# Fewer ScalarE products for VectorE's convolution taps, and GpSimd's taps dealt out in other places

## The chip, the cores and the metric

The kernel runs on one core of a Trainium2 chip. A core has five engines that run their own queues in a fixed order and wait for each other by semaphores: TensorE (PE, with its weight loads as PEld), VectorE (DVE), ScalarE (ACT), GpSimd (POOL) and SyncE (SP), which issues most transfers. Data lies in SBUF, results of TensorE in the banks of PSUM. The metric is the device time of one execution in microseconds (us).

## The reference, cut to what matters

One decoder layer over 256 positions of width 1024. Two token mixers read the same normalized input `h`: a convolution module and sparse attention with 16 heads. The change touches the convolution; the attention runs next to it in time.

```python
def conv_module(u, dw_w, dw_b, ln_g, ln_b, pw_w):
    a, gt = jnp.split(u, 2, axis=-1)
    v = a * jax.nn.sigmoid(gt)
    v = lax.conv_general_dilated(                 # depthwise, causal, 31 taps, 1024 channels
        v, dw_w[:, None, :], window_strides=(1,), padding=((CONV_WIDTH - 1, 0),), ...) + dw_b
    v = jax.nn.silu(layer_norm(v, ln_g, ln_b))
    return v @ pw_w
...
y = jax.nn.sigmoid(g_conv) * conv_out + jax.nn.sigmoid(g_attn) * nsa_out
return y @ w_out
```

Cross-attention into 256 memory tokens and a SwiGLU feed-forward part follow; the change leaves them alone.

## The kernel before

**Chunks and halves.** All weights of the first projection come in chunks of 512 KB, in the order u, kc, vc, q, ks, kw, vs, vw, ga, gc (u is the convolution's input, kc to vw the attention's keys and values, ga and gc the two gates). Each chunk is cut into a rounded high half, by ScalarE (L187), and a low half, the rest (L190). GpSimd makes the low halves of the chunks up to ga3, VectorE those of gc and what follows. TensorE multiplies high by high, high by low and low by high (L279).

**The taps.** The eight blocks of 128 channels form four chains of two blocks: 0, 2, 4 and 6. A tap multiplies a shifted view of the input (`vt`) by one weight per channel and adds it to the chain's sum. `taps_v` does this on VectorE: either as a fused multiply and add for each block (L458), or ScalarE makes the product of both blocks (L442) into one of four buffers with the tag vw, and VectorE adds it in one instruction of twice the length (L454). The sum, `yp`, lies in PSUM. `taps_g` is GpSimd's: ScalarE makes a product (L472), or GpSimd itself for taps 5 and 11 (L470), into one of the same four buffers, and GpSimd adds it (L474). Chains 0, 2 and 4 are wholly VectorE's. Of chain 6 GpSimd has taps 0 to 15 and VectorE taps 16 to 30, and L478 joins the two parts on GpSimd. Then GpSimd forms the sum for the layer norm (L662, two L664, folded by L333).

**What sets the order.** `convolve(n_v, n_g, *marks)` takes the next n_v steps of VectorE's taps and n_g of GpSimd's, puts them behind the marks (the instructions named) and gives them a priority 1500 places later, so that they fill gaps. It is called once behind each chunk's result. A scheduler then simulates the engines and writes each engine's order down; nothing is reordered on the chip. Marks, priorities and durations thus decide where a tap stands in a queue.

**Attention.** Eight pairs of heads, each in two steps. `scores` of a pair: TensorE writes the scores of the first 128 queries of both heads into one PSUM bank with the tag s0, of which there is one, and those of the later 128 into banks of the tag s. VectorE adds the bias and takes minima: four L783 read s0, four L789 the others. `weights`: ScalarE takes exponentials with their sums (L804), VectorE makes factors of the sums (L807, L809) and multiplies them in, four L812 and four L814 in turn. Then TensorE transposes the result (L825): `pt_b` into the bank s0, `pt_a` into one of the two banks "pt". The program lets pair 1's scores go ahead of pair 0's transposes. So `pt_b` of pair 0 cannot be written before the last L783 of pair 1 has read the bank, and these L783 stand behind pair 0's L812 and L814 in VectorE's queue. Behind pair 0's transposes TensorE has the next gate chunk and pair 2's scores.

**The gates.** L698 takes the gate ga out of PSUM on ScalarE; the next gate's matmuls need that bank.

Of the kernel before, what the change touches and what calls it, by code (L numbers as in the profile page):

```python
# [11 lines left out]
AF = mybir.ActivationFunctionType  # L12
# [10 lines left out]
TAPS = 31  # L23
# [78 lines left out]
def tile_hybrid_block(  # L102
# [15 lines left out]
    nc = tc.nc  # L118
# [18 lines left out]
    def small(name, shape, dt=F32, tag=None, bufs=1):  # L137
        return sb.tile(shape, dt, tag=tag or name, name=name, bufs=bufs)
# [10 lines left out]
    def aux(name, shape, tag, bufs):  # L149
        return axp.tile(shape, F32, tag=tag, name=name, bufs=bufs)  # L150

    def f(ap):
        return ap.bitcast(F32)
# [17 lines left out]
    def col(base, j):  # L171
        return ppt[:, base + j:base + j + 1]
# [22 lines left out]
    first, splits, apart = {}, {}, {}  # L195
# [25 lines left out]
    def behind(*marks):  # L221

        stack = ExitStack()
        for m in marks:
            stack.enter_context(tc.issue_after(m.ins))
        return stack
# [63 lines left out]
    def gemm(name, x, nat=False):  # L290

        ps = bank(f"ps_{name}")
        for i in range(2):
            sweep(ps, halved(name, i), x, i, nat, name in in_order)
        return ps
# [122 lines left out]
    for i in range(4):  # L418
        hs = slice(2 * i, 2 * i + 2)
        for kb in (2 * i, 2 * i + 1):  # L420
            vec = nc.vector.scalar_tensor_tensor(out=hf[:, kb], in0=xt_t[:, kb], scalar=col(PP_GMIX, kb),
                                                 in1=r1, op0=ALU.mult, op1=ALU.mult)
# [16 lines left out]
    def product_of(j, t, to):  # L439

        for i in range(2):
            nc.scalar.activation(to[:, i], vt[j + i][:, t:t + S], AF.Identity, scale=col(PP_DW + TAPS * (j + i), t),  # L442
                                 bias=col(PP_DB, j + i) if t == 0 else 0.0)

    def taps_v(j, ts, out):

        acc = aux(f"yp{j}", [P, 2, S], "pt", 2)
        product_of(j, ts[0], acc)
        for n, t in enumerate(ts[1:]):
            to = out if t == ts[-1] else acc  # L450
            if n % 2:
                pr = small(f"vw{j}_{t}", [P, 2, S], tag="vw", bufs=4)
                product_of(j, t, pr)
                nc.vector.tensor_tensor(out=to, in0=acc, in1=pr, op=ALU.add)  # L454
                yield
                continue
            for i in range(2):
                nc.vector.scalar_tensor_tensor(out=to[:, i], in0=vt[j + i][:, t:t + S], scalar=col(PP_DW + TAPS * (j + i), t),  # L458
                                               in1=acc[:, i], op0=ALU.mult, op1=ALU.add)
                yield  # L460
# [36 lines left out]
    def convolve(n_v, n_g, *marks):  # L497

        here = tc.cur_priority
        tc.cur_priority = here + 1500  # L500
        with behind(*marks):
            for _ in range(n_v):
                next(on_v, None)
            for _ in range(n_g):
                next(on_g, None)
        tc.cur_priority = here

    small("gap2", [P, 32])
    for j in range(NB):
        ps = gemm(f"u{j}", h)  # L510
        sg = small(f"sg{j}", [P, S], tag="sg", bufs=3)
        act = nc.scalar.activation(sg, ps[:, 1], AF.Sigmoid)
        vec = nc.vector.tensor_tensor(out=vt[j][:, PAD:], in0=ps[:, 0], in1=sg, op=ALU.mult)
# [41 lines left out]
    for kv, name in enumerate(("kc", "vc")):  # L555
        ps = gemm(name, h)
        zin = zins[:, kv]
        nc.vector.memset(zin[:, :, :, NCMP:], 0.0)
        for odd in range(2):
            for lo, g in ((0, 0), (64, 1)):  # L560
                at = (PP_POS if lo == 64 * odd else PP_SOP) + 16 * kv
                view = ps[lo:lo + 64, :, odd:S]
                vec = nc.vector.tensor_tensor(
                    out=zin[64 * odd:64 * odd + 64, :, g::2, 0:NCMP],
                    in0=bass.AP(tensor=view.tensor, offset=view.offset, ap=[list(view.ap[0]), [2, 16], [S, 2], [16, NCMP]]),
                    in1=ppt[lo:lo + 64, at:at + 16].unsqueeze(2).unsqueeze(3).to_broadcast([64, 16, 2, NCMP]), op=ALU.add)
        convolve(5, 0, vec)
    kcp = small("kcp", [P, GROUPS, 2, 16], F32R)
    vcs = small("vcs", [P, 2, HD], tag="sg", bufs=3)
    vals = long("vals", 12, (P, 2, HEADS * HD))  # L570
# [3 lines left out]
    def hidden():  # L574


        z_ps = aux("z_ps", [P, 64], "o", 1)
        for l in range(16):
            for kv in range(2):
                nc.tensor.matmul(z_ps[HD * kv:HD * kv + HD], lhsT=w1t[:, kv, l], rhs=zins[:, kv, l].rearrange("p g n -> p (g n)"),  # L580
                                 start=l == 0, stop=l == 15)
        zs = small("zs", [P, 64], tag="zs", bufs=2)
        nc.scalar.activation(zs, z_ps, AF.Sigmoid)
        nc.vector.tensor_tensor(out=zz[:HD, 0, :64], in0=z_ps[:HD], in1=zs[:HD], op=ALU.mult)
        nc.vector.tensor_tensor(
            out=zz[HD:, 1].rearrange("p (g r n) -> p g r n", g=GROUPS, r=4),
            in0=z_ps[HD:].rearrange("p (g n) -> p g n", g=GROUPS).unsqueeze(2).to_broadcast([HD, GROUPS, 4, 16]),
            in1=zs[HD:].rearrange("p (g n) -> p g n", g=GROUPS).unsqueeze(2).to_broadcast([HD, GROUPS, 4, 16]), op=ALU.mult)

    def compressed():  # L590

        kc_ps = aux("kc_ps", [P, GROUPS, 16], "s0", 1)
        nc.tensor.matmul(kc_ps, lhsT=ppt[:, PP_W2K:PP_W2K + P], rhs=zz[:, 0, :64].rearrange("p (g n) -> p g n", g=GROUPS),
                         start=True, stop=True)
        part(kcp[:, :, 0], kcp[:, :, 1], kc_ps[:])
        vc_ps = aux("vc_ps", [P, 2, HD], "o", 1)
        for i in range(2):
            nc.tensor.matmul(vc_ps[:, i], lhsT=zz[:, 1, i * P:i * P + P], rhs=ppt[:, PP_W2V:PP_W2V + HD],
                             start=True, stop=True)
        nc.scalar.activation(vcs, vc_ps, AF.Copy)  # L600
# [4 lines left out]
    for j in range(4):  # L605
        ps = gemm(f"q{j}", h)
        q0, q1 = ([qt[j // 2][:, 4 * (j % 2) + 2 * b + k] for b in range(2)] for k in range(2))
        for b in range(2):
            nc.scalar.activation(q0[b][0:64], ps[0:64, b], AF.Copy, scale=-0.125)
            act = nc.scalar.activation(q1[b][64:128], ps[64:128, b], AF.Copy, scale=-0.125)  # L610
        for b in range(2):
            nc.vector.scalar_tensor_tensor(out=q0[b][64:128], in0=ps[0:64, b], scalar=-0.125, in1=f(q0[b][0:64]),
                                           op0=ALU.mult, op1=ALU.subtract)
            vec = nc.vector.scalar_tensor_tensor(out=q1[b][0:64], in0=ps[64:128, b], scalar=-0.125, in1=f(q1[b][64:128]),
                                                 op0=ALU.mult, op1=ALU.subtract)
        convolve(7, 1, act, vec)
        with behind(*last):
            if j == 0:
                hidden()
            elif j == 2:  # L620
                compressed()
# [3 lines left out]
    for br, name in enumerate(("ks", "kw")):  # L625
        ps = gemm(name, h)

        for lo, g in ((0, 0), (64, 1)):
            for to in (lo, 64 - lo):
                act = nc.scalar.activation(kdh[to:to + 64, g::2, br], ps[lo:lo + 64], AF.Copy)  # L630
        for lo, g in ((0, 0), (64, 1)):
            for to in (lo, 64 - lo):
                vec = nc.vector.tensor_tensor(out=kdl[to:to + 64, g::2, br], in0=ps[lo:lo + 64],
                                              in1=f(kdh[lo:lo + 64, g::2, br]), op=ALU.subtract)
        convolve(5, 1, act, vec)


    for br, name in enumerate(("vs", "vw")):
        ps = gemm_nat(name, h)
        act = nc.scalar.activation(vst[:, :, br], ps, AF.Copy)  # L640
# [5 lines left out]
    g_ps = aux("g_ps", [P, S], "s0", 1)  # L646
    for kb in range(NB):
        nc.tensor.matmul(g_ps[64 * (kb % 2):64 * (kb % 2) + 64], lhsT=wg[:, kb], rhs=hf[:, kb], start=kb < 2, stop=kb >= NB - 2)
    sgn = small("sgn", [P, S], tag="sg", bufs=3)
    igd = small("igd", [P, HEADS, 2, 2])  # L650
    igc = small("igc", [P, 2, HEADS])
    convolve(8 * TAPS, 2, nc.scalar.activation(sgn, g_ps, AF.Copy))

# [35 lines left out]
    def gate(j, few=iter(())):  # L691

        ps = bank(f"ps_ga{j}")
        for i in range(2):
            for _ in rows(ps, halved(f"ga{j}", i), h, i):
                for _ in range(3):
                    next(few, None)
        return nc.scalar.activation(sga[:, 2 * j:2 * j + 2], ps, AF.Copy if j == 3 else AF.Sigmoid)  # L698
# [27 lines left out]
    for tb in range(2):  # L726
# [4 lines left out]
    vec = nc.vector.reciprocal(igd.rearrange("p h t b -> p t b h"),  # L731
                               sgt[:, :, HEADS:3 * HEADS].rearrange("p t (b h) -> p t b h", b=2))
    hm = cpt[:, CP_HM:CP_HM + 8].unsqueeze(2).to_broadcast([P, 8, HD])
    with behind(vec):
        for i in range(2):
            nc.vector.tensor_tensor(out=vcm[:, 8 * i:8 * i + 8], in0=vcs[:, i].unsqueeze(1).to_broadcast([P, 8, HD]), in1=hm,
                                    op=ALU.mult)
    convolve(0, TAPS, splits["ga1_0"][0])
    mark = gate(2)
    def compressed_weights(*marks):  # L740

# [699 lines left out]
```

## Time and profile before

| | |
|---|---|
| time, median of 3 runs (lowest to highest) | 543.54 us (543.37 to 545.13) |
| profiled execution, its own time | 544.06 us |
| its span, first to last instruction | 542.3 us |
| mean granted clock of TensorE | 0.991 |
| busy: PE, DVE, ACT, POOL | 527.9, 438.6, 380.4, 140.9 us |

The profile is of one execution, so sums are made against its own time. Busy time is per engine and counts no waiting. The timeline gives start and duration of each instruction and, in brackets, the idle time just ahead of it and what ended it; listed durations of neighbours on VectorE and ScalarE overlap a little. The granted clock is the share of full speed that the chip gave TensorE.

### The profile page before, as it was taken

To read this page: it belongs to the slowest core of one execution; us is meant where nothing else is said; L and a number is where in the kernel's file an instruction comes from. 1 tells how busy PE (TensorE), PEld (TensorE's weight loads), DVE (VectorE), ACT (ScalarE), POOL (GpSimd) and SP (SyncE) were. 2 spreads that over 40 slices of the span, in tenths; PEclk is the share of its full clock that TensorE was granted. 3 is DMA by queue.
4 is the path that set the end of the run, shared out by engine and by line. 5 is a ranking of instruction groups with operands and counts; after the bars stand their busy time and mean duration, and the time that the engine had idled before them with its cause. 6 is when DMAs were issued, how large, how long until landed. Compare 5 with 4: busy or idle time off the path is not lost.

```text
span 542.3 us, 11221 instructions
## 1 busy us (share of the span) xinstructions
PE 527.9 (97%) x4325; PEld 508.8 (94%) x4325; DVE 438.6 (81%) x841; ACT 380.4 (70%) x705; POOL 140.9 (26%) x101
## 2 busy tenths in 40 slices
PE   9999999999999499999999999999999999999995
PEld 8999999999999499898999999999999999988884
DVE  3885999678998999795777876498798887689996
ACT  3679895999988688789756685376465555567643
POOL 0009987888967400200001300040000000000002
PEclk9999999999999799999999999999999999999999
DMA  8946956543555144523576643438676555634502
GB/s 277 410 166 226 336 198 193 189 158 120 193 164 170 58 137 147 178 87 144 160 221 217 231 160 114 156 126 277 232 244 210 193 196 195 195 118 133 179 1 77
DMA packets 29301, 97.38 MB, mean 180 GB/s; under 512 B 3136, under 2 KB 5440, under 8 KB 28992
## 3 DMA queue, kind: packets, MB, share of 16 engines
q1 hardware_dynamic: 28672, 95.62, 52.9%
q10 hardware_dynamic: 576, 1.05, 0.5%
q8 instruction: 34, 0.56, 0.4%
q14 instruction: 19, 0.16, 0.1%
HBM read 95.41 MB, written 1.25 MB: 178 GB/s over the span
## 4 chain that ended last, share of the span: by engine, by line
PE 80%; ACT 11%; DVE 4%; DMA 3%; issue 1%; POOL 0%; SPq 0%; ACTq 0%; POOLq 0%
PE ps_f L279 22%; PE ps_u L279 8%; PE fo L1209 6%; PE ps_v L279 4%; PE ps_xq L279 4%; PE ps_pw L279 4%; PE ps_wo L279 4%; PE fos L1209 4%; ACT vw L442 3%; PE ps_gc L279 3%; PE ps_xo L279 3%; PE ps_k L279 2%; PE ps_q L279 2%; PE ps_xo L1094 2%; ACT vw L472 1%; DMA xtsq<-in_xt_dram 1%
## 5 line engine op out<-in xcount | busy, mean ns | idle before, releaser
L458 DVE SCALAR_TENSOR_TENSOR yp<-vt,ppt,yp 128x256 f32<-128x256 f32 x104 | 47.9, 484 | 3.9 <-ACT yp L442 2.5
L1278 POOL TENSOR_TENSOR x<-xs,gf 128x512 f32<-128x512 f32 x2 | 2.5, 1293 | 168.3 <-issue 168.3
L442 ACT ACTIVATE vw<-vt,ppt 128x256 f32<-128x256 f32 x104 | 44.6, 499 | 0.1
L279 PE MATMUL ps_f<-g,f_1h 128*128 128x256 f32 x352 | 44.4, 277 | 0.0
L279 PE MATMUL ps_f<-g,f_0h 128*128 128x256 f32 x352 | 43.9, 277 | 0.0
L279 PEld LDWEIGHTS ps_f<-g,f_1h 128*128 128x128 f32 x352 | 41.9, 188 | 0.0
L279 PEld LDWEIGHTS ps_f<-g,f_0h 128*128 128x128 f32 x352 | 41.8, 188 | 0.0
L187 ACT ACTIVATE f_0h<-f 128x1024 fp32r<-128x1024 f32 x22 | 23.3, 1058 | 17.8 <-issue 15.5
L804 ACT ACTIVATE p<-p,mins 128x128 f32<-128x128 f32 (+1 forms) x64 | 28.3, 444 | 10.2 <-DVE mins L783 10.0
L454 DVE TENSOR_TENSOR yp<-yp,vw 128x512 f32<-128x512 f32 x48 | 33.1, 695 | 2.2 <-ACT vw L442 0.9
L190 DVE TENSOR_TENSOR f_1l<-f,f_1h 128x1024 fp32r<-128x1024 f32 x22 | 27.3, 1246 | 4.9 <-ACT f_1h L187 4.9
L190 DVE TENSOR_TENSOR f_0l<-f,f_0h 128x1024 fp32r<-128x1024 f32 x22 | 27.3, 1243 | 3.9 <-ACT oxh L324 2.2
L187 ACT ACTIVATE f_1h<-f 128x1024 fp32r<-128x1024 f32 x22 | 23.2, 1059 | 8.2 <-PE ps_f L279 7.5
L279 PE MATMUL ps_f<-g,f_1l 128*128 128x256 f32 x176 | 23.6, 276 | 0.0
L1168 DVE TENSOR_TENSOR ab<-ps_f,rf 128x512 f32<-128x512 f32 x22 | 15.2, 689 | 10.4 <-PE ps_f L279 10.4
L279 PE MATMUL ps_f<-g,f_0l 128*128 128x256 f32 x176 | 23.6, 276 | 0.0
L474 POOL TENSOR_TENSOR yt<-yt,vw 128x512 f32<-128x512 f32 x15 | 20.2, 1348 | 12.0 <-ACT vw L472 10.8
L190 POOL TENSOR_TENSOR u_0l<-u,u_0h 128x1024 fp32r<-128x1024 f32 x5 | 12.0, 2406 | 40.0 <-ACT u_0h L187 40.0
L279 PEld LDWEIGHTS ps_f<-g,f_1l 128*128 128x128 f32 x176 | 21.6, 188 | 0.0
L279 PEld LDWEIGHTS ps_f<-g,f_0l 128*128 128x128 f32 x176 | 21.6, 188 | 0.0
L988 POOL COPY acc<-s_wo 128x256 f32<-128x256 f32 x1 | 0.7, 653 | 71.7 <-ACT s_wo L984 71.7
L1170 ACT ACTIVATE sl<-ab 128x256 f32<-128x256 f32 x22 | 9.1, 417 | 11.3 <-DVE ab L1168 11.3
(827 smaller groups left out, 1673.7 us busy)
## 6 DMA issues: line engine op xcount, KB each, us to landing
f<-in_wst_dram SPq DMA_DIRECT2D x44, 512.0 KB, 4.1
u<-in_wst_dram SPq DMA_DIRECT2D x14, 512.0 KB, 7.2
for<-in_wfo_dram SPq DMA_DIRECT2D x14, 512.0 KB, 3.8
q<-in_wst_dram SPq DMA_DIRECT2D x8, 512.0 KB, 5.8
ga<-in_wst_dram SPq DMA_DIRECT2D x8, 512.0 KB, 3.6
gc<-in_wst_dram SPq DMA_DIRECT2D x8, 512.0 KB, 3.5
v<-in_wst_dram SPq DMA_DIRECT2D x8, 512.0 KB, 4.1
pw<-in_wst_dram SPq DMA_DIRECT2D x8, 512.0 KB, 4.6
```

Of the source, the lines that this page charges most:

```text
L187: copies = [nc.scalar.activation(hi[:, at:at + n], w[:, at:at + n], AF.Copy) for at in range(0, shape[1], n)]
L190: low = eng.tensor_tensor(out=lo[:, at:at + n], in0=w[:, at:at + n], in1=f(hi[:, at:at + n]), op=ALU.subtract)
L279: mm = nc.tensor.matmul(ps[:, b], lhsT=lhsT, rhs=rhs, start=row + b + kb == 0, stop=kb == NB - 1 and row == 2 and b == 1)
L442: nc.scalar.activation(to[:, i], vt[j + i][:, t:t + S], AF.Identity, scale=col(PP_DW + TAPS * (j + i), t), bias=col(PP_DB, j + i) if t == ...
L454: nc.vector.tensor_tensor(out=to, in0=acc, in1=pr, op=ALU.add)
L458: nc.vector.scalar_tensor_tensor(out=to[:, i], in0=vt[j + i][:, t:t + S], scalar=col(PP_DW + TAPS * (j + i), t), in1=acc[:, i], op0=ALU.mu ...
L474: nc.gpsimd.tensor_tensor(out=y, in0=y, in1=pr, op=ALU.add)
L804: exp.append(nc.scalar.activation(t, t, AF.Exp, scale=-1.0, bias=mins[:, hd, qb, br:br + 1], accum_out=sums[:, hd, qb, br:br + 1]))
L1094: nc.tensor.matmul(qs[:, b], lhsT=parts[m, 1][wi][:, k, cs], rhs=x[xi][:, 4 + k], start=False, stop=k == 3 and row == 2 and b == 1)
L1168: nc.vector.tensor_tensor(out=ab, in0=ps, in1=rf.unsqueeze(1).to_broadcast([P, 2, S]), op=ALU.mult)
L1170: silu = nc.scalar.activation(sl, ab[:, 0], AF.Silu)
L1209: mm = nc.tensor.matmul(o[:, cs], lhsT=t[x], rhs=w[y][:, cs], start=start and n == 0, stop=stop and n == 2)
```

## The change

VectorE's chains take a product from ScalarE where n % 3 is 2, n being the tap's place behind the first: every third tap and no longer every second. The calls of `convolve` behind the chunks kc, vc, q, ks and kw take more steps of VectorE's taps and one or two of GpSimd's; the call behind the gate's logits takes all of GpSimd's steps that are left, and the later call behind ga1 is gone. (In the orders below, lines of the changed kernel behind that call are lower by one: L811 is L812 of before.)

```diff
@@ taps_v
-            if n % 2:
+            if n % 3 == 2:
                 pr = small(f"vw{j}_{t}", [P, 2, S], tag="vw", bufs=4)
@@ behind kc and vc
-        convolve(5, 0, vec)
+        convolve(8, 1, vec)
@@ behind q0 to q3
-        convolve(7, 1, act, vec)
+        convolve(8, 2, act, vec)
@@ behind ks and kw
-        convolve(5, 1, act, vec)
+        convolve(6, 1, act, vec)
@@ behind the gate's logits
-    convolve(8 * TAPS, 2, nc.scalar.activation(sgn, g_ps, AF.Copy))
+    convolve(8 * TAPS, TAPS, nc.scalar.activation(sgn, g_ps, AF.Copy))
@@ ahead of gate(2)
-    convolve(0, TAPS, splits["ga1_0"][0])
```

VectorE's queue around the normalizing of pair 0, before (yp is the sum in PSUM, here of chain 4; yt takes its last add):

```order
L190 TENSOR_TENSOR gc_0l<-gc_0_2614,gc_0h 128x1024
L458 SCALAR_TENSOR_TENSOR yp_1398<-vt_357,ppt,yp_1398 128x256
L454 TENSOR_TENSOR yt<-yp_1398,vw_30_1985 128x512
L807 SCALAR_TENSOR_TENSOR sums<-sums,igd 128x8
L809 RECIPROCAL sums<-sums 128x8
L812 TENSOR_SCALAR p_0_2280<-p_0_2280,sums 128x256
L814 TENSOR_SCALAR p_0_2265<-p_0_2265,sums 128x128
...
L814 TENSOR_SCALAR p_0_2265<-p_0_2265,sums 128x128
L783 ISA p_1_2439,mins<-s_1_2438,nb_2435 128x128
```

and after:

```order
L454 TENSOR_TENSOR yp_1467<-yp_1467,vw_27_1965 128x512
L458 SCALAR_TENSOR_TENSOR yp_1467<-vt_357,ppt,yp_1467 128x256
L806 SCALAR_TENSOR_TENSOR sums<-sums,igd 128x8
L458 SCALAR_TENSOR_TENSOR yp_1467<-vt_357,ppt,yp_1467 128x256
L808 RECIPROCAL sums<-sums 128x8
L458 SCALAR_TENSOR_TENSOR yp_1467<-vt_357,ppt,yp_1467 128x256
L811 TENSOR_SCALAR p_0_2244<-p_0_2244,sums 128x256
L813 TENSOR_SCALAR p_0_2229<-p_0_2229,sums 128x128
...
L813 TENSOR_SCALAR p_0_2229<-p_0_2229,sums 128x128
L458 SCALAR_TENSOR_TENSOR yp_1467<-vt_357,ppt,yp_1467 128x256
L454 TENSOR_TENSOR yt<-yp_1467,vw_30_1973 128x512
L782 ISA p_1_2403,mins<-s_1_2402,nb_2399 128x128
```

Chain 4's last add stood ahead of L807; now it stands behind the last L813, ahead of pair 1's first L782, with an L458. Two more L458 stand on either side of L808. Between the rows shown three more pairs of L812 and L814 (L811 and L813) follow.

GpSimd's queue from its last low half (ga_1l of ga3) on, before:

```order
L190 TENSOR_TENSOR ga_1l<-ga_1_2317,ga_1h 128x1024
L474 TENSOR_TENSOR yt<-yt,vw_8_1989 128x512
L474 TENSOR_TENSOR yt<-yt,vw_9_1993 128x512
L470 TENSOR_SCALAR vw_11_2178<-vt_358,ppt 128x256 x2
L474 TENSOR_TENSOR yt<-yt,vw_10_2174 128x512
L474 TENSOR_TENSOR yt<-yt,vw_11_2178 128x512
L474 TENSOR_TENSOR yt<-yt,vw_12_2182 128x512
L474 TENSOR_TENSOR yt<-yt,vw_13_2186 128x512
L662 TENSOR_TENSOR ysum<-yt 128x512
L474 TENSOR_TENSOR yt<-yt,vw_14_2190 128x512
L474 TENSOR_TENSOR yt<-yt,vw_15_2194 128x512
L478 TENSOR_TENSOR yt<-yt,part_364 128x512
```

and after:

```order
L190 TENSOR_TENSOR ga_1l<-ga_1_2281,ga_1h 128x1024
L474 TENSOR_TENSOR yt<-yt,vw_13_1914 128x512
L474 TENSOR_TENSOR yt<-yt,vw_14_1977 128x512
L662 TENSOR_TENSOR ysum<-yt 128x512
L474 TENSOR_TENSOR yt<-yt,vw_15_1981 128x512
L478 TENSOR_TENSOR yt<-yt,part_364 128x512
L664 TENSOR_TENSOR ysum<-ysum,yt 128x512 x2
L333 TENSOR_TENSOR ysum<-ysum 128x256
```

Behind the last low half stood eight L474 and an L470 pair; three L474 are left. The others moved up between the low halves of q to ga3. The join L478 and the layer norm's sum follow in both.

ScalarE's queue around pair 0's exponentials, before:

```order
L804 ACTIVATE p_0_2265,sums<-p_0_2265,mins 128x128 x3
L187 ACTIVATE gc_1h<-gc_1_2509 128x1024
L804 ACTIVATE p_0_2265,sums<-p_0_2265,mins 128x128
L472 ACTIVATE vw_12_2182<-vt_358,ppt 128x256 x2
L187 ACTIVATE gc_0h<-gc_0_2614 128x1024
L472 ACTIVATE vw_13_2186<-vt_358,ppt 128x256 x2
L698 ACTIVATE sga<-ps_ga_2286 128x512
L804 ACTIVATE p_0_2280,sums<-p_0_2280,mins 128x256 x2
```

and after:

```order
L472 ACTIVATE vw_14_1977<-vt_358,ppt 128x256 x2
L187 ACTIVATE gc_0h<-gc_0_2443 128x1024
L472 ACTIVATE vw_15_1981<-vt_358,ppt 128x256 x2
L698 ACTIVATE sga<-ps_ga_2163 128x512
L803 ACT_TABLE_LOAD
L803 ACTIVATE p_0_2229,sums<-p_0_2229,mins 128x128 x4
L187 ACTIVATE gc_1h<-gc_1_2473 128x1024
L187 ACTIVATE gc_0h<-gc_0_2578 128x1024
L698 ACTIVATE sga<-ps_ga_2250 128x512
L803 ACTIVATE p_0_2244,sums<-p_0_2244,mins 128x256 x2
```

The L472 pairs that stood between the exponentials of the earlier and the later queries have moved up; the two high halves of gc (L187) and L698 remain between them.

## The prediction

> **What bounds the kernel now.** I read three views in this order: the page's first part and the waits of PE, to see which engine sets the end and where it stops; then the timelines of PE, DVE and POOL around the one stop; then the granted clock by stretch. First the page's busy shares and, from the waits grouped by engine, PE's longest (total, times, longest):
>
> ```profile
> PE 527.9 (97%) x4325; PEld 508.8 (94%) x4325; DVE 438.6 (81%) x841; ACT 380.4 (70%) x705; POOL 140.9 (26%) x101
> PE pt_b L825 <- DVE mins L783: 7.0, 1, 7.0
> ```
>
> PE is busy 97% of the span, and half of what is missing is one wait: the transposes of attention pair 0 (pt_b) stand still until DVE has read the scores of pair 1 (L783) out of the PSUM bank that both use. ACT, DVE and POOL can lose work without any gain wherever PE does not wait. The timeline of PE around that wait, with the next pair's same work below it (start, duration):
>
> ```profile
> 175.01 1.07 PE L279 MATMUL ps_gc<-hh,gc_1h 128*128 128x256 f32 x8
> 183.05 1.08 PE L825 MATMUL pt_b<-cpt,p 128*128 128x128 f32 x4 [6.97 <-DVE mins L783]
> ...
> 188.59 0.40 PE L770 MATMUL s<-kdh,qt 128*128 128x512 f32 x1
> ...
> 193.63 1.08 PE L279 MATMUL ps_gc<-hl,gc_1h 128*128 128x256 f32 x8
> 194.55 0.60 PE L825 MATMUL pt_b<-cpt,p 128*128 128x128 f32 x4
> ...
> 195.86 0.38 PE L670 MATMUL mu<-ysum,ones 128*128 128x256 f32 x1
> ```
>
> From the stall's end to the next scores takes 188.59 - 183.05 = 5.54 us. At full clock the twelve transposes take 195.86 - 194.55 = 1.31 us and the two gemm groups of eight 0.91 each (such a group from 193.63 to 194.55), 3.13 in all. So 2.41 us more are lost behind the stall. The windows show why (length, busy time of PE, PEld, DVE, ACT and POOL, then the granted clock PEclk, third from the right):
>
> ```profile
> 176.00:181.00 5.00, 0.08 (x1) 0.00 (x0) 5.00 (x8) 1.10 (x2) 4.69 (x5) 1.00 0.00 0
> 181.00:183.00 2.00, 0.00 (x0) 0.00 (x0) 2.00 (x10) 0.70 (x4) 1.70 (x2) 0.54 0.00 0
> 183.00:188.00 5.00, 4.95 (x24) 4.98 (x25) 4.89 (x17) 4.83 (x17) 0.00 (x0) 0.50 0.36 112
> ```
>
> PE idles from 176.08, the clock is 1.00 until 181 and about 0.5 from there to 188: it fell some 5 us into the idle stretch. The place is worth 6.97 + 2.41 = 9.4 us.
>
> What held DVE is in its groups of 175:182, with POOL busy, against 183:200, with POOL idle (busy us, mean ns):
>
> ```profile
> L814 DVE TENSOR_SCALAR p<-p,sums 128x128 f32<-128x128 f32 x4 | 5.2, 1298 | 0.0
> ...
> L812 DVE TENSOR_SCALAR p<-p,sums 128x256 f32<-128x256 f32 x4 | 1.4, 353 | 0.0
> L814 DVE TENSOR_SCALAR p<-p,sums 128x128 f32<-128x128 f32 x4 | 1.1, 285 | 0.0
> L807 DVE SCALAR_TENSOR_TENSOR sums<-sums,igd 128x8 f32<-128x8 f32 x2 | 0.3, 159 | 0.0
> ```
>
> and the timelines of DVE and POOL there:
>
> ```profile
> 174.11 0.85 DVE L807 SCALAR_TENSOR_TENSOR sums<-sums,igd 128x8 f32<-128x8 f32 x1 [0.58 <-ACT p L804]
> ...
> 175.23 1.17 DVE L812 TENSOR_SCALAR p<-p,sums 128x256 f32<-128x256 f32 x1
> ...
> 181.98 0.28 DVE L783 CUSTOM_DVE_ANT_0 p<-s,nb 128x128 f32<-128x128 f32 x1
> ...
> 182.61 0.28 DVE L783 CUSTOM_DVE_ANT_0 p<-s,nb 128x128 f32<-128x128 f32 x1
> ...
> 174.95 2.63 POOL L474 TENSOR_TENSOR yt<-yt,vw 128x512 f32<-128x512 f32 x2
> ...
> 179.12 2.85 POOL L664 TENSOR_TENSOR ysum<-ysum,yt 128x512 f32<-128x512 f32 x2
> ```
>
> The eight normalizing instructions take 181.98 - 175.23 = 6.75 us beside POOL's adds. Four L814 lose 1.01 us each against the later pair, the first L812 0.82: 4.9 us in all. L807 loses 0.85 - 0.16, 0.7 more. They seem to start only where an instruction of POOL ends.
>
> **The change part by part.** The shares move first (page, groups):
>
> ```profile
> L458 DVE SCALAR_TENSOR_TENSOR yp<-vt,ppt,yp 128x256 f32<-128x256 f32 x104 | 47.9, 484 | 3.9 <-ACT yp L442 2.5
> ...
> L442 ACT ACTIVATE vw<-vt,ppt 128x256 f32<-128x256 f32 x104 | 44.6, 499 | 0.1
> ...
> L454 DVE TENSOR_TENSOR yp<-yp,vw 128x512 f32<-128x512 f32 x48 | 33.1, 695 | 2.2 <-ACT vw L442 0.9
> ```
>
> Chains 0, 2 and 4 have 30 taps behind the first: n % 2 gave ScalarE 15 of them, n % 3 gives 10. The 15 of chain 6 go from 7 to 4. So 18 taps leave ScalarE: 36 activations fewer, 18.0 us by 499 ns, for 36 more L458 on DVE (17.4 us by 484 ns) less 18 L454 (12.5 us by 695 ns): +4.9 us for DVE. Listed durations overlap by about 0.1, so by starts it is nearer +3. None of this is on PE's path by itself.
>
> L458's 484 ns is a mean over 104, most of them beside a busy POOL, so L458 does not wait for POOL as L814 does; if each of the 36 lost 1.0 us like L814, DVE would carry 36 us more. [...]
> DVE's extra is covered by the chunks' matmuls until 175, and would be paid in full if DVE were late there by itself.
>
> Second, POOL's taps. In the order of POOL shown ahead, five L474 and one L470 pair fewer stand behind its last low half (ga_1l). That last low half and what it must be early for:
>
> ```profile
> 152.79 2.46 POOL L190 TENSOR_TENSOR ga_1l<-ga,ga_1h 128x1024 fp32r<-128x1024 f32 x1
> 158.56 1.58 POOL L474 TENSOR_TENSOR yt<-yt,vw 128x512 f32<-128x512 f32 x1 [3.31 <-ACT vw L472]
> ...
> 164.01 1.11 PE L279 MATMUL ps_ga<-hh,ga_1l 128*128 128x256 f32 x8
> ```
>
> Five L474 (about 1.25 without a wait) and an L470 pair (some 0.9) more ahead of it are 7.2 us. POOL's busy time, the last before PEclk, leaves room for part of that:
>
> ```profile
> 100.00:130.00 30.00, 30.00 (x266) 30.00 (x265) 24.50 (x51) 29.69 (x61) 24.91 (x13) 1.00 0.48 159
> 150.00:175.00 25.00, 25.00 (x206) 24.31 (x205) 22.41 (x48) 21.48 (x51) 16.93 (x13) 1.00 0.54 175
> ```
>
> From 100 to 130 it is idle 30 - 24.91 = 5.1 us; I let the new work fill 4 of them. So the last low half ends near 158.5, not 155.25, and PE wants it at 164.0. That delay costs nothing; 5.5 us of cover remain. Behind it POOL has three L474, an L662 and an L478, at 1.3 to 1.6 us each about 7 us; with waits they are done near 168 to 170, the first L664 soon after. The second L664 needs chain 4's last add (DVE's L454 into yt). Before, that add stood ahead of L807; in the new order it stands behind the last L814. So this L664 and L333 can't run beside the normalizing steps: the order excludes it, whatever the durations.
>
> Third, the start of it on DVE. The gc splits, L736 and L807 meet a busy POOL elsewhere now. L190 on DVE has these two durations, beside POOL and nearly alone:
>
> ```profile
> 159.30 1.93 DVE L190 TENSOR_TENSOR gc_1l<-gc,gc_1h 128x1024 fp32r<-128x1024 f32 x1
> ...
> 164.13 0.28 DVE L783 CUSTOM_DVE_ANT_0 p<-s,nb 128x128 f32<-128x128 f32 x1
> ...
> 168.78 1.23 DVE L190 TENSOR_TENSOR gc_1l<-gc,gc_1h 128x1024 fp32r<-128x1024 f32 x1 [1.43 <-ACT gc_1h L187]
> ```
>
> A split beside POOL takes 0.7 us longer. Before, two met POOL ahead of L783; now three and the two L736 may, which I count as 2.5 us more. Against that three L458 (0.4 each by starts) have moved from ahead of this L783 to behind it, and some 0.9 us come from an earlier start. That puts pair 0's first L783 at 164.5, 0.4 late. On ScalarE this group lies between pair 0's first exponentials and its last four, which L807 waits for (168.5 to 171.8):
>
> ```profile
> L472 ACT ACTIVATE vw<-vt,ppt 128x256 f32<-128x256 f32 x4 | 1.8, 494 | 0.0
> ```
>
> All four have moved ahead of the exponentials, so that these end near 172 and L807 is paced by DVE's own splits and taps. By the rows of its queue it comes near 173.2, 0.9 us earlier.
>
> **The sum at the stall.** DVE reads pair 1's scores earlier by 0.9 (L807's start) + 4.9 + 0.7 (waits for POOL), later by three L458 and one L454 that now stand between L807 and L783 (3 x 0.48 + 0.70, rows above, 2.2): 4.3 us, ending at 178.6, not 182.9. PE would come to the stall 0.4 us earlier, near 175.7, since this wait goes with an earlier L698:
>
> ```profile
> 172.16 1.00 PEld L279 LDWEIGHTS ps_gc<-hh,gc_0h 128*128 128x128 f32 x8 [0.42 <-ACT sga L698]
> ```
>
> So it stalls 3 us, not 7. The clock fell 5 us into the stall; at 3 us I take it not to fall.
>
> [...]
>
> PE alone would gain 4.0 + 2.4 + 0.4 = 6.8 us. But DVE is behind next. From 182 to 213.3 it is saturated, and pair 3's turn comes close:
>
> ```profile
> 182.00:213.30 31.30, 30.25 (x233) 28.44 (x234) 30.31 (x109) 27.24 (x76) 0.73 (x1) 0.90 0.45 143
> 213.09 0.28 DVE L783 CUSTOM_DVE_ANT_0 p<-s,nb 128x128 f32<-128x128 f32 x1
> 214.26 0.64 PE L825 MATMUL pt_b<-cpt,p 128*128 128x128 f32 x4
> ```
>
> DVE (30.31 busy of 31.30) ends that L783 some 0.96 us before PE uses it. PE can therefore come earlier there by DVE's 4.3 and those 0.96: 5.3 us. After pair 3 DVE waits for PE, so the gain stays. The profiled execution, 544.06 us (span 542.3 and 1.76 around it), would be 538.8; it is 0.52 above the median, which gives 543.54 - 5.3 = 538.2.
>
> **Rivals.** (B) All of the stall goes: ScalarE's 18 us free VectorE earlier, too, and DVE is 3 us ahead at pair 0 already. For it: the 2.5 and 0.9 us that DVE waited for ScalarE's products in the groups. Against: gc splits follow the transfers and DVE's extra work eats that. Worth 6.97 + 2.41 + 0.42 = 9.8 us, 533.7.
>
> [...] If POOL runs 10 us later than I replayed, L474 or L478 stand beside the normalizing steps again; half the waits return (2.5 us), the stall is over 5 us and the clock falls. Gain 4.3 - 2.5 = 1.8, without the 0.96 since PE at half clock no longer presses on pair 3, so 541.7. For it: POOL waited 3.3 us for one ScalarE product at 158.56. Against: the second L664 is out by order, and 10 us is more than its work left.
>
> (E) The change shifts work but not the end: DVE's extra 4.9 us, paid between 150 and 175 where it is busy 22.41 of 25 us (window above), cancels the 4.3: 543.5. Against: with POOL's low halves early enough, DVE waits for chunks there too, and three L458 moved out of the stretch.
>
> (D) Slower: POOL's tap 13 now stands behind the last low half, and ScalarE's product for tap 14 must wait for its buffer, with gc1's high half, L698 and the exponentials queued behind it. By my replay L698 ends 0.9 us before PE needs its bank. If tap 13 ends 4 us or more after 160, the exponentials move to 176 to 178, POOL's last adds meet the normalizing steps once more, and L783 ends at 186: 3 us more than now, 546.6. It decides from about 164 on.
>
> **How the numbers follow.** Forecast 538.2 with 0.47 (its own range 537 to 540); B 0.15; C 0.18; E 0.11; D 0.09. 0.3% is 1.6 us, about what a measurement can tell here. C lies just past it: 0.13 of its 0.18 count as faster. Faster: 0.47 + 0.15 + 0.13 = 0.75; same: 0.05 + 0.11 = 0.16; slower 0.09. The range holds forecast, B and C, 0.80 together: 533.5 to 542.6.
>
> **What would show it.** PE's wait for L783 near 3 us and PEclk at 1.00 throughout it; L814 in pair 0 near 0.28 us, not 1.3; POOL idle from about 170 until chain 4's last add on DVE; L783 of pair 1 ending near 178.6; a new short wait of PE for L783 at pairs 1 to 3. ACT with 36 instructions fewer and DVE with 18 more. The forecast is wrong if L814 is still 1.3 us, if L807 comes after 174, if PE waits for a low half of POOL, or if the wait at pair 3 is over 2 us.

## The result, and the profile after

The changed kernel takes 537.65 us (median of 4, 537.15 to 538.63), the kernel before 544.34 us beside it (median of 4). The ratio is 0.9878, with a 95% interval of 0.985 to 0.9907. The same program run again later (e10) gave 0.9862 (0.9841 to 0.9883). The prediction was 538.2 us. The profiled execution took 537.44 us with a span of 535.6 us, 6.7 us less than before. In the runs of the experiments below, the kernel before lay between 541 and 546 us, so differences under 1 us between kernels that did not run side by side say nothing; where two of them are compared closely, I read the positions in the profiles. In the run called e8, two of the four executions and the profile were disturbed and are not used.

The page's busy line of the changed kernel, then PE's waits:

```profile
PE 525.7 (98%) x4325; PEld 506.1 (94%) x4325; DVE 438.8 (82%) x859; ACT 367.4 (69%) x669; POOL 139.2 (26%) x101
PE pt_b L824 <- DVE mins L782: 1.1, 2, 0.9
...
PE pc_ps L902 <- ACT ptt_a L827: 1.0, 1, 1.0
```

VectorE has 18 instructions more and no more busy time (438.8 for 438.6), ScalarE 36 fewer and 13 us less. The 7.0 us wait has become two waits of 1.1 together, and a wait for ScalarE is new. PE's timeline shows where the 6.7 us are:

```profile
174.99 1.11 PE L279 MATMUL ps_gc<-hh,gc_1h 128*128 128x256 f32 x8
177.01 0.63 PE L824 MATMUL pt_b<-cpt,p 128*128 128x128 f32 x4 [0.91 <-DVE mins L782]
...
180.23 0.40 PE L769 MATMUL s<-kdh,qt 128*128 128x512 f32 x1
...
186.70 0.63 PE L824 MATMUL pt_b<-cpt,p 128*128 128x128 f32 x4 [0.20 <-DVE mins L782]
...
192.91 0.66 PE L902 MATMUL pc_ps<-cpt,nsc 128*128 128x128 f32 x4 [1.04 <-ACT ptt_a L827]
```

PE reaches the stall at the same time as before (176.1). The wait is 6.06 us shorter (6.97 to 0.91). From there to pair 2's scores takes 3.22 us, not 5.54: the half clock, 2.32 us, is gone. That is 8.4 us. Behind it 1.7 us are given back: 0.5 up to pair 1's transposes, 1.2 at `pc_ps`, the transposes of the compressed weights, which wait for ScalarE. ScalarE's queue has three high halves of the chunks v (weights of the cross-attention) ahead of the copies `ptt_a` that PE waits for; the first of the three, and the copies:

```profile
189.43 1.05 ACT L187 ACTIVATE v_0h<-v 128x1024 fp32r<-128x1024 f32 x1
...
192.28 1.06 ACT L827 ACTIVATE ptt_a<-pt_a 128x512 f32<-128x512 f32 x2
```

From there to the end the two kernels run 6.6 to 6.7 us apart.

The clock's windows (PEclk is third from the right) confirm the second term:

```profile
175.00:177.00 2.00, 1.10 (x10) 0.92 (x9) 1.97 (x11) 0.74 (x4) 0.84 (x1) 1.00 0.01 4
177.00:178.00 1.00, 0.99 (x9) 1.00 (x10) 1.00 (x7) 1.00 (x7) 0.92 (x2) 1.00 0.00 0
178.00:183.00 5.00, 5.00 (x41) 4.83 (x40) 4.93 (x16) 5.00 (x13) 0.24 (x1) 1.00 0.49 147
```

And the timelines of DVE and POOL show why VectorE is early:

```profile
171.93 0.16 DVE L806 SCALAR_TENSOR_TENSOR sums<-sums,igd 128x8 f32<-128x8 f32 x1
172.05 0.49 DVE L458 SCALAR_TENSOR_TENSOR yp<-vt,ppt,yp 128x256 f32<-128x256 f32 x1
...
172.98 0.35 DVE L811 TENSOR_SCALAR p<-p,sums 128x256 f32<-128x256 f32 x1
173.24 0.28 DVE L813 TENSOR_SCALAR p<-p,sums 128x128 f32<-128x128 f32 x1
...
174.81 0.48 DVE L458 SCALAR_TENSOR_TENSOR yp<-vt,ppt,yp 128x256 f32<-128x256 f32 x1
175.33 0.69 DVE L454 TENSOR_TENSOR yt<-yp,vw 128x512 f32<-128x512 f32 x1
175.94 0.28 DVE L782 CUSTOM_DVE_ANT_0 p<-s,nb 128x128 f32<-128x128 f32 x1
...
166.43 1.29 POOL L664 TENSOR_TENSOR ysum<-ysum,yt 128x512 f32<-128x512 f32 x1
176.16 1.27 POOL L664 TENSOR_TENSOR ysum<-ysum,yt 128x512 f32<-128x512 f32 x1 [8.44 <-DVE yt L454]
```

GpSimd is silent from 167.7 to 176.16, as the order wanted it, and the eight normalizing instructions take 174.81 - 172.98 = 1.83 us, not 6.75.

### The profile page after: what moved, and what is told of

Its sections match the earlier page's. It is cut to its first block, busy times and chain, and to the rows that moved or that the text cites. A ratio compares the mean times of both kernels' runs of the same rounds, so it can differ in the third digit from the quotient of the medians.

```text
span 535.6 us, 11193 instructions
## 1 busy us (share of the span) xinstructions
PE 525.7 (98%) x4325; PEld 506.1 (94%) x4325; DVE 438.8 (82%) x859; ACT 367.4 (69%) x669; POOL 139.2 (26%) x101
## 4 chain that ended last, share of the span: by engine, by line
PE 88%; DVE 5%; ACT 3%; DMA 3%; issue 0%; SPq 0%; ACTq 0%; DVEq 0%
PE ps_f L279 22%; PE ps_u L279 8%; PE fo L1208 6%; PE ps_v L279 4%; PE ps_q L279 4%; PE ps_xq L279 4%; PE ps_pw L279 4%; PE ps_wo L279 4%; PE fos L1208 4%; PE ps_ga L279 3%; PE ps_xo L279 3%; PE ps_k L279 2%; PE ps_xo L1093 2%; DMA xtsq<-in_xt_dram 1%; PE o L848 1%; DMA mem_t<-in_memt_dram 1%
## 5 line engine op out<-in xcount | busy, mean ns | idle before, releaser
L458 DVE SCALAR_TENSOR_TENSOR yp<-vt,ppt,yp 128x256 f32<-128x256 f32 x138 | 61.9, 482 | 3.7 <-ACT yp L442 2.0
L187 ACT ACTIVATE f_0h<-f 128x1024 fp32r<-128x1024 f32 x22 | 23.3, 1061 | 19.1 <-issue 15.5
L442 ACT ACTIVATE vw<-vt,ppt 128x256 f32<-128x256 f32 x68 | 29.7, 499 | 1.7 <-DVE yp L454 1.3
L187 ACT ACTIVATE f_1h<-f 128x1024 fp32r<-128x1024 f32 x22 | 23.2, 1061 | 8.5 <-PE ps_f L279 7.9
L454 DVE TENSOR_TENSOR yp<-yp,vw 128x512 f32<-128x512 f32 x31 | 21.4, 692 | 0.7
L474 POOL TENSOR_TENSOR yt<-yt,vw 128x512 f32<-128x512 f32 x15 | 19.4, 1293 | 5.3 <-ACT vw L472 4.2
```

Source lines behind the costliest of these rows:

```text
L187: copies = [nc.scalar.activation(hi[:, at:at + n], w[:, at:at + n], AF.Copy) for at in range(0, shape[1], n)]
L474: nc.gpsimd.tensor_tensor(out=y, in0=y, in1=pr, op=ALU.add)
```

## The experiments

**e1, the swap alone.** Every third product, GpSimd's and VectorE's dealing as before.

```diff
 (kernel before)
-            if n % 2:
+            if n % 3 == 2:
```

> Only the first part of the change: every third product from ScalarE, GpSimd's taps dealt out as before. GpSimd's queue still has eight adds of taps behind its last low half. Theory (the gain is the end of GpSimd's contention with pair 0's normalizing): L814 of pair 0 still takes about 1.3 us beside GpSimd, PE still waits 4 to 7 us for L783, the time is 541.5 to 544.5 us. Rival (the gain is ScalarE's relief, 18 us of it): L807 starts at 172 as in the changed kernel, PE's wait is under 2 us, the time is 537.5 to 539.5 us.

Measured: 546.28 us, ratio 1.0042 (1.0024 to 1.0061): slower. Both expectations missed the place. VectorE starts L807 at 169.4 and PE's wait for L783 is only 0.83 us, as the rival said, though GpSimd is beside it: L807 takes 1.21 us and two of pair 0's four L814 take 1.3, so the theory's mark is half there too. But PE then waits elsewhere; PE, DVE, ACT and POOL of this kernel:

```profile
176.84 0.63 PE L825 MATMUL pt_b<-cpt,p 128*128 128x128 f32 x4 [0.83 <-DVE mins L783]
...
182.45 1.11 PE L825 MATMUL pt_a<-cpt,p 128*128 128x128 f32 x4 [4.55 <-ACT ptt_a L828]
...
183.52 0.68 DVE L454 TENSOR_TENSOR yt<-yp,vw 128x512 f32<-128x512 f32 x1
...
179.43 2.49 ACT L472 ACTIVATE vw<-vt,ppt 128x256 f32<-128x256 f32 x6
181.82 0.57 ACT L828 ACTIVATE ptt_a<-pt_a 128x512 f32<-128x512 f32 x1
...
165.11 1.66 POOL L474 TENSOR_TENSOR yt<-yt,vw 128x512 f32<-128x512 f32 x1 [12.28 <-ACT vw L472]
```

A fused tap is two steps of `convolve`, an added product one; with more fused taps the same number of steps does fewer taps. So chain 4 falls behind and ends at 184.2, not before 174. Its sum lies in one of the two banks "pt". Pair 0's second transposes must then use the bank of the first, and wait until ScalarE has copied it out, behind three pairs of products that were late too. In that stall the clock falls to half as well (0.50 from 180 to 186). The larger numbers of steps for VectorE in the change are thus needed by the swap; without them it costs 2 us.

**e2, the dealing alone.** The changed kernel with ScalarE's products as before.

```diff
 (changed kernel)
-            if n % 3 == 2:
+            if n % 2:
```

> Only the second part: GpSimd's taps dealt out early and the call behind ga1 gone, ScalarE makes every second product as before. GpSimd's queue has three adds of taps behind its last low half, as in the changed kernel, but chain 4's last add stands ahead of the normalizing again, so that the second L664 may run beside it. Theory (contention): GpSimd is done with its taps before the normalizing, L813 takes 0.28 to 0.6 us, the time is 537.5 to 540.5 us. Rival (ScalarE's relief): ScalarE, still full between 100 and 150 us, holds the products back, PE's wait stays above 4 us and the time is 541.5 us or more.

Measured: 539.54 us, ratio 0.9918 (0.9888 to 0.9948), two thirds of the gain, as the contention theory expected. PE waits 2.23 us; its timeline:

```profile
178.58 0.63 PE L824 MATMUL pt_b<-cpt,p 128*128 128x128 f32 x4 [2.23 <-DVE mins L782]
179.04 1.87 PE L824 MATMUL pt_a<-cpt,p 128*128 128x128 f32 x8
```

and the clock's windows:

```profile
178.50:179.00 0.50, 0.42 (x4) 0.45 (x5) 0.50 (x3) 0.50 (x4) 0.00 (x0) 1.00 0.00 0
179.00:179.50 0.50, 0.50 (x5) 0.50 (x4) 0.50 (x3) 0.50 (x5) 0.00 (x0) 0.57 0.00 0
180.00:181.00 1.00, 1.00 (x7) 1.00 (x6) 1.00 (x6) 0.83 (x3) 0.00 (x0) 0.50 0.00 0
```

The clock fell after 2.2 us of idle time, half a microsecond after work had begun again. What the swap adds in the full change is an L806 2.3 us earlier (171.93, here 174.27, where it waited for ScalarE's exponentials), and with it the clock. These exponentials were late because VectorE was: pair 0's first L782 came at 167.91, in the changed kernel at 165.12, and ScalarE waited 5.1 us for it.

**e3, GpSimd's adds put back.** Only these lines are added to the changed kernel (they change chain 0's sum in its last bits).

```diff
 (changed kernel, layer_norm_sum, behind the first L664)
+    copy of pair 0's factors to a small tile on GpSimd   # starts when L808 ends
+    for op in (add, subtract) * 2:                       # four, as large as L474
+        yt[:, 0:2] = yt[:, 0:2] op yt[:, 2:4]            # on GpSimd
```

> The changed kernel with the suspected cause put back by itself: behind the first L664, GpSimd copies pair 0's finished factors (so it starts when L808 ends) and then runs four adds of L474's size (chain 0's sum plus and minus chain 2's, twice), beside pair 0's normalizing. Order and work of the other engines stay. Theory (VectorE's normalizing waits for GpSimd's instruction): the eight normalizing instructions take 5 to 6.5 us, not 1.8, pair 1's last L782 comes 3.5 to 4.5 us later, PE's wait grows from 0.9 to about 5 us, and the time is 541 to 544 us, at the upper end if the clock falls. Rival (the gain has another source): the adds go by unnoticed, 537.2 to 538.2 us.

Measured: 542.57 us, ratio 0.9972 (0.9953 to 0.999). The groups of DVE from 172 to 179 (busy us, mean ns):

```profile
L821 DVE TENSOR_SCALAR p<-p,sums 128x128 f32<-128x128 f32 x4 | 4.2, 1053 | 0.0
L819 DVE TENSOR_SCALAR p<-p,sums 128x256 f32<-128x256 f32 x4 | 2.5, 616 | 0.0
```

and the timelines of POOL and PE:

```profile
172.66 5.59 POOL L670 TENSOR_TENSOR yt<-yt 128x512 f32<-128x512 f32 x4
...
180.90 1.09 PE L832 MATMUL pt_b<-cpt,p 128*128 128x128 f32 x4 [4.90 <-DVE mins L790]
```

The eight normalizing instructions take 6.05 us (172.66 to 178.71), L783's counterpart comes 3.9 us later, the stall is 4.9 us, the clock halves (0.50 from 181 to 186). Every number lies where the theory had it. Four adds on an otherwise idle engine undo 5 of the 6.7 us. This is the cause shown by itself.

**e4, PE kept busy in the stall of the kernel before.**

```diff
 (kernel before, turned("b0"))
+    for _ in range(36): matmul(idle, lhsT=ones, rhs=ones)   # 128x128, nobody reads it
```

> The kernel before, with 36 matmuls of 128x128 (into a bank that is free, read by nobody) ahead of pair 0's transposes, so that PE is busy for the first 4 us of its 7 us wait; VectorE's order is untouched. The wait's end is still set by VectorE at about 182.9. It asks what the half clock behind the stall costs. If the clock stays full and VectorE is the next bound, as the prediction has it (0.96 us ahead of PE at pair 3): the time is about 1.0 us shorter, 542.3 to 543.3, and PE waits for L783 at later pairs. If the half clock is a cost of its own: 2.4 us shorter, 541 to 541.5. If the clock falls all the same: no change.

The 36 take 8.2 us, not 4, and end after VectorE was done, a fault in my sizing. Measured: 545.46 us, ratio 1.0024 (1.0006 to 1.0042). PE:

```profile
175.62 8.20 PE L827 MATMUL idle<-ones 128*128 128x128 f32 x72
183.66 0.60 PE L831 MATMUL pt_b<-cpt,p 128*128 128x128 f32 x4
...
186.80 0.40 PE L770 MATMUL s<-kdh,qt 128*128 128x512 f32 x1
```

The outcome is none of the three expected. The clock stayed at 1.00, and from the transposes to the next scores it took 3.14 us, 2.40 less than the kernel before: the price of the half clock, as read in the prediction. Yet nothing of it reached the end: PE waited 1.41 us at `pc_ps` for ScalarE's copy of pair 1's transposes, and `pc_ps` stood at 199.76, where it was 199.58 before. So the first bound behind the stall was not VectorE at pair 3.

**e4b and e4c, half as many, and with ScalarE's queue changed.** The second moves two high halves of the chunks v behind those copies.

```diff
 (e4b)
-    for _ in range(36):
+    for _ in range(18):
 (e4c, e4b and)
-            first["v0_0"] = first["v0_1"] = first["v1_0"] = copies[3],
+            first["v0_0"] = copies[3],
+            first["v0_1"] = first["v1_0"] = copies[5],
```

> The kernel before with 18 instead of 36 matmuls ahead of pair 0's transposes: by e4's 8.2 us for 36 they take 4.1 us and end near 180, 3 us before VectorE is done, so the wait's end is VectorE's again (182.6 to 183.1). Theory (the half clock's 2.4 us can't be had in the kernel before, because PE then waits at pc_ps for ScalarE's copies behind three high halves of v): clock full, pair 2's scores at 186.2, but pc_ps at 199.3 to 199.8 as before, time within 0.5 us of the kernel before. Rival (the half clock is a cost of its own): 2 us or more shorter.

> The same with the two high halves of v put behind the copies too. Theory (ScalarE's queue at pc_ps kept the gain from the end): pc_ps comes 1 us or more earlier than in the run with 18 matmuls alone, the time is 1.0 to 2.4 us under the kernel before. Rival (VectorE's chain binds): no more than 0.5 us.

e4b: 545.30 us, ratio 1.0016 (1.0 to 1.0033); e4c: 544.78 us, 1.0011 (0.9993 to 1.003). e4b's timeline of PE, then its window at the stall's end:

```profile
175.96 4.18 PE L827 MATMUL idle<-ones 128*128 128x128 f32 x36
183.14 0.83 PE L831 MATMUL pt_b<-cpt,p 128*128 128x128 f32 x4 [3.00 <-DVE mins L783]
```

```profile
183.00:184.00 1.00, 0.86 (x6) 0.89 (x7) 1.00 (x5) 1.00 (x7) 0.00 (x0) 0.72 0.00 0
```

The wait left is 3.0 us, and the clock fell all the same, at the end of it. So e4b does not say what a full clock is worth. In e4c `pc_ps` comes at 198.04, 2.1 us before e4b's 200.13, and PE no longer waits there (0.85 us in e4b; of the rest, 0.95 lies ahead of it, since PE's stall for VectorE ended that much earlier in e4c); but at pair 3 it waits for VectorE:

```profile
213.51 0.63 PE L831 MATMUL pt_b<-cpt,p 128*128 128x128 f32 x4 [0.91 <-DVE mins L783]
```

That is the bound of the prediction, 0.96 us behind PE. It stands right behind ScalarE's. The time decides for e4c's rival, no gain; but the clock fell in e4c as well (mean 0.993, PE idle 1.95 us), so it does not say what VectorE alone would leave.

**e7, the same two high halves in the changed kernel.** The diff is e4c's second.

> The changed kernel with two high halves of the chunk v (v0's second, v1's first) put behind ScalarE's copies of pair 1's transposes (ptt_a), which they stood ahead of. In the changed kernel PE waited 1.04 us at pc_ps for that copy. Theory (after the change the ScalarE queue between pair 1's exponentials and these copies is the next bound): that wait goes or falls under 0.2 us, the time is 0.8 to 1.0 us under the changed kernel's 537.65, so 536.6 to 537.0. Rival (VectorE binds right behind, as at pair 3 in the prediction): the time stays at 537.3 to 538.

Measured: 538.41 us, ratio 0.9897 (0.9876 to 0.9918), no faster than the changed kernel. The wait of 1.04 us at `pc_ps` is gone (it starts at 191.26, in the changed kernel at 192.91), and two new ones stand at pair 3:

```profile
206.23 0.61 PE L356 MATMUL rn_l<-ones,ssum 128*128 128x2 f32 x4 [0.39 <-DVE ssum L333]
207.16 0.63 PE L824 MATMUL pt_b<-cpt,p 128*128 128x128 f32 x4 [0.33 <-DVE mins L782]
```

The place was right, the gain was not: waits for VectorE take 0.72 us of the 1.04, the rival's case, though the time lies a little above the rival's 537.3 to 538 as well.

**e5, chain 4 back to every second product** (with e7's edit).

```diff
 (e7)
-            if n % 3 == 2:
+            if n % 2 if j == 4 else n % 3 == 2:
```

> The kernel with the later high halves of v, and chain 4 alone again takes every second product from ScalarE (5 products more for ScalarE, which has idle time from 155 to 162; 5 adds for 10 fused taps on VectorE). Chain 4's last add then stands ahead of the normalizing. Theory (what is left of PE's first wait, 0.9 us, is VectorE's taps between L806 and L782, 2.0 us): the wait falls under 0.4 us, the time is 0.4 to 0.9 us under that kernel's. Rival (ScalarE's load or the second L664, now free to run beside the normalizing, takes it back): no shorter, up to 1 us longer.

Measured: 539.23 us, ratio 0.9903 (0.9884 to 0.9922), about 0.8 us over e7's. PE's wait is 1.84 us. DVE and POOL:

```profile
172.98 0.69 DVE L454 TENSOR_TENSOR yt<-yp,vw 128x512 f32<-128x512 f32 x1
...
173.85 1.34 DVE L813 TENSOR_SCALAR p<-p,sums 128x128 f32<-128x128 f32 x1
...
173.81 1.29 POOL L664 TENSOR_TENSOR ysum<-ysum,yt 128x512 f32<-128x512 f32 x1 [5.13 <-DVE yt L454]
```

The rival's second half: with chain 4 done ahead of the normalizing, the second L664 runs beside it, and L813 takes 1.34 us; the eight instructions take 3.38 us where e7 has 1.84. L806 also comes 0.84 us later than in e7 (172.33 for 171.49), so the edit's cost is not that add alone. Where the add stands in VectorE's queue is part of the change's gain; how large a part this run does not separate.

**e8 and e11, VectorE's share of the change alone.** The swap with its larger numbers of steps; GpSimd's numbers and its late call as before.

```diff
 (kernel before)
-            if n % 2:
+            if n % 3 == 2:
-        convolve(5, 0, vec)         # kc, vc
+        convolve(8, 0, vec)
-        convolve(7, 1, act, vec)    # q
+        convolve(8, 1, act, vec)
-        convolve(5, 1, act, vec)    # ks, kw
+        convolve(6, 1, act, vec)
```

> The changed kernel's share for VectorE (every third product from ScalarE, and its larger numbers of VectorE's steps behind the chunks), with GpSimd's numbers and its late call as before: eight adds of taps stand behind its last low half. Chain 4 ends ahead of the normalizing, so the transposes find their second bank free, unlike in the run with the swap alone. Theory (GpSimd's late taps beside the normalizing make the stall): L814 takes 0.8 to 1.3 us again, PE waits 3 to 6 us for L783, the time is 541.5 to 544.5 us. Rival (with VectorE's steps dealt out, ScalarE's relief is enough): PE waits under 2 us, 537.5 to 539.5 us.

> The kernel with the swap and VectorE's numbers of steps, GpSimd's numbers and late call as before, once more, since the profile of the first was disturbed. The first gave some 540.5 us, under the 541.5 to 544.5 that I expected. New reading: with ScalarE relieved, GpSimd's products come early although its adds stand as late in its queue as before, so that only the two L664 meet the normalizing. It expects: the adds of taps 8 to 15 done by about 173, L664 beside the first two or three normalizing instructions (L807 0.8 to 1.0, L812 about 1.2, L814 0.8), PE waits 1.5 to 3.5 us for L783 and the clock falls late or not; 539.5 to 541.5 us. If instead L814 stays at 0.28 throughout and the time is the same, GpSimd is not what is left between this kernel and the changed one.

e8 gave 540.5 us from two executions (0.9917, 0.9893 to 0.9941); e11, on another chip, 542.01 us from six, ratio 0.9964 (0.995 to 0.9978). I go by e11; why the two differ stays open. e11's DVE, POOL and PE:

```profile
169.27 1.70 DVE L190 TENSOR_TENSOR gc_1l<-gc,gc_1h 128x1024 fp32r<-128x1024 f32 x1 [2.62 <-ACT gc_1h L187]
...
174.77 0.97 DVE L807 SCALAR_TENSOR_TENSOR sums<-sums,igd 128x8 f32<-128x8 f32 x1
...
176.02 1.19 DVE L812 TENSOR_SCALAR p<-p,sums 128x256 f32<-128x256 f32 x1
177.12 0.81 DVE L814 TENSOR_SCALAR p<-p,sums 128x128 f32<-128x128 f32 x1
...
174.43 2.62 POOL L664 TENSOR_TENSOR ysum<-ysum,yt 128x512 f32<-128x512 f32 x2
...
180.30 1.08 PE L825 MATMUL pt_b<-cpt,p 128*128 128x128 f32 x4 [4.92 <-DVE mins L783]
```

The new reading holds in kind: with ScalarE relieved, GpSimd's taps are done at 172, though they stand as late in its queue as before, and only the two L664 meet the normalizing: 2.2 us on L807, L812 and L814. The wait is 4.9 us, not the 1.5 to 3.5 that I gave; e8's first expectation (3 to 6 us, 541.5 to 544.5) had these two numbers, though not its L814, of which only the first was slow. Besides, L807 comes at 174.77: a split waits 2.6 us for a high half behind GpSimd's products on ScalarE, which had itself waited 3.0 and 0.8 us for GpSimd to take earlier products, and both splits then run beside GpSimd (1.70 and 1.92 us, in the changed kernel 1.23 and 1.22). With GpSimd's taps dealt out early, as in the changed kernel, neither is there.

**e9 and e10, a trial to do better, and the changed kernel beside it.** e9 is e7 with two of the eight normalizing instructions of pairs 1 to 3 on ScalarE.

```diff
 (e7, weights)
+    if hp in (1, 2, 3) and k == 1:
+        nc.scalar.activation(p1[k][:, br], p1[k][:, br], AF.Copy, scale=sums[:, hd, 1, br:br + 1])
+    else: (VectorE's L811 as it was)
```

> The changed kernel with the later high halves of v and two of the eight normalizing instructions of pairs 1 to 3 on ScalarE (as a copy with a scale), 0.26 us each off VectorE, 0.4 us each onto ScalarE. Theory (VectorE's queue up to pair 3 bounds what is left): PE's waits for L782 at pairs 1 and 3 (0.2 and 0.33 us) and for L333 (0.39) shrink together by 0.5 us or more, the time is 0.5 to 1.0 us under that kernel without it. Rival (ScalarE's queue gets the wait instead): PE waits for ScalarE's copies or scales, no gain.

> The changed kernel itself, next to the others on the same chip, for comparing with them: 537 to 538.6 us, ratio 0.985 to 0.991, PE's wait for pair 1's L782 at 0.5 to 1.5 us.

e9: 536.98 us, ratio 0.9861 (0.9835 to 0.9886); e10: 537.52 us, 0.9862 (0.9841 to 0.9883). They can't be told apart. PE's waits at pairs 1 and 3 are gone in e9, but pair 0's is 1.43 us where e10's is 0.66, and PE waits 0.57 us for a copy of ScalarE. None of these versions beats the changed kernel.

## Why the prediction was right, point by point

**The place and the cause** were right. e3 shows the contention by itself, e2 and e5 show it come and go with GpSimd's adds. None of the signs of being wrong appeared.

**VectorE's sum** had 4.3 us; it was 6.04 (pair 1's first L783 at 181.98, now 175.94). Its terms: 4.9 + 0.7 us of waits for GpSimd, measured 6.75 - 1.83 = 4.92 and 0.85 - 0.16 = 0.69, exact. The taps moved in between, 2.2, measured 1.93 (0.80 ahead of L811, 1.13 behind L813). L807's start, 0.9, measured 2.18: this term was mis-sized. These make 5.86; the other 0.18 are steps around L807 and L809 that the taps now fill (0.43 us, now 0.25). I had L807 paced by VectorE's splits beside a busy GpSimd; GpSimd was done by 167.7 with the first L664 too, which I had put behind 168 to 170, and the splits at 168.1 and 169.7 took 1.23 and 1.22 us, alone. Pair 0's first L783 came at 165.12, 1.0 late, where I had 0.4: the splits and L736 ahead of it took 3.2 us longer than before, not 2.5, most of it in one split of 4.10 us (before 1.23) beside two instructions of GpSimd.

**GpSimd's low halves** were not late: the last, for ga3, ended at 154.97, not at the 158.5 that I feared. GpSimd has no gap between 99.2 and 156.2 now, so the new work filled more of its idle time than I had allowed.

**The stall** was 0.91 us for 3. The step "at 3 us I take the clock not to fall", an estimate from the one fall in the kernel before (5.1 us into the stall), was wrong, though it did no harm: in e2 it fell at 2.2 us of idle, in e4b at 3.0. With a stall of 3 us, as I forecast, the half clock would probably have stayed in part, as in those two runs (in e2, 4.81 us from the transposes to the next scores, 1.6 more than here). The clock was kept at a stall of 0.91 us (and at 1.4 in e9 and 1.8 in e5), shorter than forecast: to that extent the term of 2.4 us came out by luck. PE did not come to the stall 0.4 us earlier, as I had it, but at the same time. The wait for L698 had held its next matmul back by only 0.15 us (0.38 from the matmul ahead to it, now 0.23), and pair 1's scores began 0.16 later.

**"DVE is behind next"** was wrong in the place and right in kind. I added 0.96 us to VectorE's shift at pair 0, as though it kept that shift up to pair 3. It gained another microsecond on the way (the last L783 that pair 3's transposes wait for, at 213.09, now 206.07: 7.02). What bound first was ScalarE's queue ahead of the copies for `pc_ps`, 1.04 us, which I had not looked at. With that removed (e4c, e7) VectorE at pair 3 stands behind it with 0.3 to 0.9 us. Two near bounds in place of one gave 6.7 in the spans, not 5.3.

**The number** is closer than the working. The forecast gain was 5.3 us, the measured one 6.7: 8.4 came free at the stall where I had 6.8, and 1.7 of it was lost at bounds of which I had named one, in another place. The times, 538.2 and 537.65, differ by less than the gains because the kernel before measured 544.34 us beside the changed one, 0.8 above the 543.54 that I started from. That is luck.

**The rivals.** B asked for VectorE to be 3 us ahead at pair 0; it was a microsecond late there, and yet nearly all of the stall went. Of its price of 9.8 us, 8.4 came at the stall; the bounds behind took 1.7 of that. C, the rival with GpSimd 10 us later than replayed (541.7), needed GpSimd beside the normalizing; it was not there, and e5, e11 and e3 show what it costs when it is. E did not come about: VectorE's busy time did not even rise (438.8 for 438.6): the waits for GpSimd that went, 5.6 us, had counted as busy. D did not come about: tap 13 ended at 156.2.

## What to carry to other kernels

Look at which small instructions of VectorE have several durations in one profile, and at what GpSimd does meanwhile: here four adds of 1.4 us (5.59 together, e3), work for an engine with 74% idle time, cost 5 us at the end. GpSimd's work should lie where VectorE runs instructions that did not slow down beside it (here L458, a mean of 0.48 us, and L454, 0.69, beside GpSimd and without it), or where nothing waits for VectorE, and an order that makes it impossible there (an input that comes later) is surer than one that makes it early. A shift of work between two engines changes how much of it a fixed number of steps does; the swap alone, without the new numbers, was slower. Before a freed wait is credited in full, every next wait up to the place where the slack begins has to be bounded, here ScalarE's copies for `pc_ps` too (1.04 us).

## What the runs showed of the hardware that was not expected

The granted clock fell after shorter idle times than I had read from one profile: 5.1 us into the stall in the kernel before, but 4.0 in e3, 3.3 in e4b, 3.1 in e11 and 2.7 in e2; in e4b and e2 that was after PE had begun again (idle 3.0 and 2.2 us), and so in e4c, after only 1.95 us of idle time. In e1 it fell 1.4 us into the long stall, which had a stall of 0.8 us and 1.1 us of work ahead of it. After one stall of 0.9 us (changed kernel), 1.4 (e9) or 1.8 us (e5) it did not fall in the profiled executions. It stayed at half for about 3.4 us in e2, e4b and e4c, and for about 6.8 in the kernel before, in e1, e3 and e11. One of the changed kernel's four executions (538.63 us) has a mean clock of 0.993, the profiled one 0.999; e2's and e4c's profiled executions, with one stretch of 3.4 us at half clock each, also have 0.993, so the clock may still fall there at times. No profile shows it. What sets the moment of the fall and these two lengths, none of the runs shows.

A matmul of 128x128 by 128x128 in float32 stands in e4's profile as two instructions, 0.114 us each (72 for 36 matmuls, in 8.20 us).
